# Reordering ScalarE and VectorE work around three places of a decoder trunk: feed of the down projection, Q/K additions, weight sums of the second feed-forward

## The chip, the cores and the metric

The kernel runs on one core of one Trainium2 chip. The metric is the device time of one execution in microseconds (us); the time of a kernel is the median of several runs. TensorE (PE) multiplies matrices and writes into eight banks of PSUM, VectorE (DVE) and ScalarE (ACT) do elementwise work and read those banks, GpSimd (POOL) and SyncE (SP) here mostly issue transfers (DMAs). Each engine runs its own instructions in the order in which the program emitted them and waits on semaphores for the others.

## The reference: what is computed

Two layers on a sequence of 1024 tokens of width 1024, all in float32. Layer 0 mixes tokens with a gated short convolution, layer 1 with a dilated attention of 16 heads (three branches, windows 128, 512 and 2048 with dilation 1, 4 and 16). Each mixer is followed by a SwiGLU feed-forward of inner width 2816, and a norm ends the network:

```python
for i in range(DEPTH):
    h = rms_norm(x, mix_norm[i])
    x = x + (short_conv_mixer if i % 2 == 0 else dilated_attention_mixer)(h, ...)
    h = rms_norm(x, ffn_norm[i])
    x = x + (silu(h @ w_gate[i]) * (h @ w_up[i])) @ w_down[i]
return rms_norm(x, final_norm)
```

## The kernel before

**Precision.** Each float32 operand is split into a high half `hi`, a rounded copy made by ACT, and a low half `lo = t - hi`, a subtraction made by DVE. A product is then three matmuls: hi by hi, hi by lo, lo by hi. Weights are split in `split` (ACT at L147, DVE at L148), activations in `Strassen.hi` (L578, L579) or `operand` (L896, L897). In `Strassen.mm` the matmuls of lines L586, L587 and L588 are the three; L588 is the one that needs the weight's low half.

**Seven products instead of eight.** The large projections use Winograd's form of Strassen's scheme. A unit `u` is a pair of 128-column weight slabs; its products have the numbers m = 1, 2, 6, 5, 7, 3, 4 (`WINOGRAD`). A product (u, m) multiplies a sum of weight blocks (made on DVE by `add_pair`, L208, named `combo`) with operand m, a sum of activation blocks that all units share (tiles `b`). Four pairs of tiles by three make twelve matmuls of 512 columns. The results are collected in banks: ACT saves a bank into a tile `part` (`save`, L592), DVE adds a bank to a tile (`add`, L596). `first(u)` is such an addition; it frees the bank of product (u, 2). Behind the first units of the feed-forward some products go a level deeper (`add_deep`, `deeper`; numbers above `DEEPER`, 256 columns, lines L678 to L681; their sums are L252).

**Order.** The order is written out by hand. `unit_order` lists the products; `products` walks through it. In front of the matmuls of each product `take` emits the splits of the weights of the next two or three products (`ahead`; `ensure` emits up to a given place), and after them come the saves and additions, a hook if there is one, and `filled(n)`, where n is the place in the order. `filled` calls `start(n)` of the stage, which makes the operands and sums at fixed places, then the feed, then `idle`. In the feed-forward the order begins (0,1), (1,1), (0,2), (1,2), (2,1), (2,2), (3,1), (3,2), (0,6), (1,6), (0,7), (1,7), (0,4), (1,4), (0,5), (1,5), (2,6), (0,3), and ends with unit 21: (21,1), (20,3), (21,6), (21,5), (21,7), deep 1, 2, 5, 6, (21,3), deep 7, 3, 4. The last product of a stage is followed by the down projection (`down`).

**Memory.** Large tiles are pages of one pool of 41 (weights, slabs `raw`, operands `b`, loaded tiles `hin`); halves of pages come from a pool of 20. A new tile gets the page that was given back longest ago, and its first writer waits for the last reader of the old tile. Transfers of slabs and `hin` go through SP in order.

**The three places.** (1) `feed(0)` (L774) brings the operands of the first down projection: at each step it allocates and loads three tiles of the next m (L786) and splits the three loaded at the step before (L578 three times, then L579 three times). `run` steps it at four places of the last unit (L864). (2) In `QueryKey.mix` the order begins (0,1), (1,1), (0,2), (1,2), (2,1), (2,2), (3,1), (3,2), (4,1). Behind (1,2) the hook `gather` starts the sums of squares of the norm (ACT L489, DVE L493); behind (3,1) the hook `spread` adds them over the partitions with four matmuls (L501). `first(0)` and `first(1)` are in `start` at n = 3 and 4, each ahead of the weights that `ensure` emits there. (3) `Swiglu.feed_forward` and the output projection before it (`group1` in `into_ffn`). The output projection runs in two halves of columns, j = 0 and 1, each over n = 0 to 7. The sums of weights of unit 0 (`combos[i, 0]`, three DVE instructions for m = 6 and 7) are made in j = 1, those of unit 1 in `start` at n = 0, between the steps of the norm's sums. `second_half` makes the operands of the second half of the sequence in six steps: step 1 multiplies by the norm and makes operands 7 and 6, step 2 subtracts, step 3 makes operand 4, step 4 subtracts, step 5 makes operand 5, step 6 operand 3. After step 1 they are called at n = 5, 7, 8, 10 and 12. The first feed-forward, behind the convolution, has some of these steps at other places, so several numbers depend on `self.key` or `i`, which is 0 for the first feed-forward and 1 for the second.

Of the kernel before, what the change touches and what calls it, by code (L numbers as in the profile page):

```python
# [30 lines left out]
DEEP, DEEPER = (2, 4), 10  # L31
# [72 lines left out]
def trunk(ctx: ExitStack, tc: tile.TileContext, x, gains_in, cwi, ck, cwo, wqkv, wo, relb,  # L104
# [60 lines left out]
    combos, raw_base, sums_of = {}, {}, {}  # L165
# [227 lines left out]
    def run(*gens):  # L393
        for _ in zip(*gens):
            pass
        for g in gens:
            for _ in g:
                pass
# [153 lines left out]
    class Strassen:  # L552
# [292 lines left out]
        def run(self, start, hooks={}):  # L845

            self.base = op_state[1]
            last = self.nu - 1

            def filled(n):  # L850
                start(n)
                if self.key != CONV:
                    self.now = n + 1
                    i = self.order.index((3, 4))
                    if n == i - 10:
                        prep.append(self.deepen(2))
                    if n == i - 1:
                        prep.append(self.deepen(4))
                    for p in prep:
                        next(p, None)  # L860
                if self.key == CONV:
                    self.below(n, last)
                else:
                    if self.order[n] in [(last, m) for m in (1, 6, DEEPER + 1, DEEPER + 4)]:  # L864
                        next(feed, None)
                    if self.order[n] == (last, DEEPER + 7):
                        ensure(self.at(last, DEEPER + 4) + 4)
                self.idle(n)

            prep = []  # L870
            if self.key == CONV:
                self.products(filled, hooks)
                self.first_tiles()
                return
            feed = self.feed(0)
            self.products(filled, hooks)
            for c in range(0, self.pairs, self.chunk):
                self.down(c, 0, feed)
                feed = self.feed(c + self.chunk) if c + self.chunk < self.pairs else self.feed_last()
                self.down(c, 4, feed)  # L880
            run(feed)
# [255 lines left out]
    class QueryKey(Conv):  # L1137
# [43 lines left out]
        def mix(self):  # L1181
            norm = self.norm
            prep = self.differences()
            stats = norm.stats(0, S)
            x12 = []

            def start(n):
                if n == 0:
                    ensure(self.at(2, 2))
                    next(prep)  # L1190
                elif n == 1:
                    ensure(self.at(3, 1))
                    next(prep)
                elif n == 3:
                    self.first(0)
                    ensure(self.at(4, 1))
                elif n == 4:
                    self.first(1)
                    ensure(self.at(4, 2))
                elif n == 5:  # L1200
                    ensure(self.at(0, 6))
                elif n == 6:
                    ensure(self.at(1, 6))
                elif n == 7:
                    next(prep)
                elif n == 8:
                    self.first(2)
                    ensure(self.at(0, 7))
                elif n == 9:
                    next(prep)  # L1210
                    next(prep)
                elif n in (10, 12):
                    next(prep)
                elif n == 11:
                    next(prep)
                    self.first(3)
                elif n == 13:
                    self.first(4)
                elif n == 14:
                    next(prep, None)  # L1220
                elif n == 20:
                    self.ahead = 3

            def gather():
                next(stats)
                next(stats)

            def spread():
                run(stats)
                rms = dram.tile([1, S], F32, name="rms")  # L1230
                norm.r = consts.tile([128, KT], F32, name="scales")
                nc.gpsimd.dma_start(rms, norm.rstd[0:1, :])
                nc.gpsimd.dma_start(norm.r, bass.AP(rms.tensor, rms.offset, [[1, 128], [128, KT]]))
                self.ready = True

            def load():
                for k in range(4):
                    x12.append(half_page("x12"))
                    nc.sync.dma_start(x12[k], spill[k][:, half(1)])

            def last_operand():
                self.b[8] = [None] * 4
                for k in range(4):
                    self.operand(8, k, k, x12[k])

            def filled(n):
                start(n)
                self.idle(n)

            norm.flush()  # L1250
            self.base = op_state[1]
            ensure(self.at(0, 2))
            self.products(filled, {(1, 2): gather, (3, 1): spread, (QK_PAIRS - 1, 1): load, (QK_PAIRS - 1, 7): last_operand})
            self.h = [[self.b[1 + 7 * h * (k < 4) + (1 + h) * (k > 3)][k % 4] for k in range(KT)] for h in range(2)]
            self.step(len(self.waiting) + 1)


    class Swiglu(Strassen):
# [111 lines left out]
        def feed_forward(self, stats, last_step, after, final=None):  # L1370
            prep = []

            def start(n):
                if n == 0:
                    last_step()
                    for m in (6, 7):
                        next(stats)
                        combos[self.key, 1](m)
                    ensure(self.at(3, 1))
                if n == self.key + 1:  # L1380
                    combos[self.key, 2](6)
                    ensure(self.at(0, 6))
                elif n == self.key + 2:
                    run(stats)
                    prep.append(self.second_half())
                    next(prep[0])
                    nc.scalar.activation(scratch, eps, AF.Silu)
                    ensure(self.at(1, 6))
                elif n == 4:
                    ensure(self.at(1, 7))  # L1390
                elif n in (5, 7, 8, 10, 12):
                    next(prep[0], None)
                if n in (8, 24):
                    self.ahead = 3 if n == 8 else 2

            self.run(start)
            key = ("d", self.key)
            if final:
                final(key, self.plain, self.hid)
                return  # L1400
            for n in range(KT):
                add_to_x(n, both(take(key + (n,), 2 if n > 3 else 1), self.plain, self.hid))
                after(n)
# [22 lines left out]
    def into_ffn(i, norm):  # L1426
# [10 lines left out]
        def group1(key, ks, acts):  # L1437
            def added(j, n):

                if j == 0 and n > 2:  # L1440
                    if 3 < n < KT - 2:
                        ensure(op_state[1] + 1)
                    ensure(first_op + n - 2)
                elif j and n in (2, 3):
                    ensure(first_op + n + 4)

            def between(j, n):
                nc.scalar.dma_start(spill[n][:, half(j)], X[n][:, half(j)])
                if j == 0:
                    if n == 2:  # L1450
                        load_raw(raw_base[i] + 3)
                    elif n == 3:
                        if not i:
                            nc.scalar.activation(less, gains, AF.Copy, scale=-1.0)
                    elif n == 4 and last_part:
                        last_part.pop()()
                    elif n == KT - 1:
                        norm.flush()
                    return
                if n == i:  # L1460
                    pre.append(norm.stats(0, HALF))
                    for m in (6, 7):
                        next(pre[0])
                        combos[i, 0](m)
                elif n == i + 1:
                    run(pre.pop())
                    pre.append(sw.first_half())
                for k in (((), (0,), (1,), (2, 3), (4,)), ((), (), (0, 1), (2, 3), (4,)))[i][n] if n < 5 else (n,):
                    step(k)

            by_columns((key, 1), ks, acts, HALVES, lambda n, c: norm.chained(n, *c, i), between,
                       AO_WIDE if key == "ao" else 4, added=added)

# [593 lines left out]
```

## Time and profile before

| what | value |
|---|---|
| median of 3 runs | 2099.22 us (2099.01 to 2099.78) |
| the profiled execution | 2098.44 us |
| its span, first to last instruction | 2096.6 us |
| granted clock of TensorE | 0.999 |
| busy: PE, DVE, ACT, POOL | 99%, 84%, 49%, 12% of the span |
| DMA | 300.72 MB, mean 143 GB/s |

Busy times are shares of the span. In a timeline a row gives the start, the duration from the first to the last instruction merged into it, engine, line, operation, tiles written and read, shape, the count, and in brackets the idle time of the engine before it and what ended it. Instructions of one engine overlap a little, so the count times the pitch, not times the duration of one, gives the time of a row. In the table of waits a row gives who waited for whom, the sum in us, how often, and the longest. A row of the table of stretches gives the stretch, its length, and for each engine the busy time and the number of instructions in it, then clock, share of the DMA engines and GB/s.

### The profile page before, as it was taken

Reading aid. Unit: us, or ns where it says so; the run is one execution under the profiler, and the core shown is the slowest. Engines: PE = TensorE matmul, PEld = TensorE weight load, DVE = VectorE, ACT = ScalarE, POOL = GpSimd, SP = SyncE. Lnnn points to the kernel's source line nnn. Section 1 sums busy time; section 2 is a strip of 40 time slices with the busy share of each in tenths; the row PEclk is TensorE's granted clock in tenths of the full one; section 3 lists DMA queues with packets and bytes.
Section 4 is the critical chain, followed back from the end, with each engine's and each line's share of the span. In section 5 each row is a group of like instructions: output and inputs, shape, how many; then the busy total and the mean of one; then the engine's idle time right before and its main releaser. Section 6 shows DMA issues by size and latency. Waiting matters only on the chain.

```text
span 2096.6 us, 30790 instructions
## 1 busy us (share of the span) xinstructions
PE 2076.3 (99%) x10978; PEld 1788.3 (85%) x10978; DVE 1757.3 (84%) x3308; ACT 1022.6 (49%) x1892; POOL 247.4 (12%) x352
## 2 busy tenths in 40 slices
PE   9999999999999999999999999999999999999998
PEld 7788888888888888888889999998788888888887
DVE  8898769988888788968985888987998888888886
ACT  8333427444444455445544666665544434456433
POOL 1000000110101010010223333211001011001000
PEclk9999999999999999999999999999999999999999
DMA  7232643233333467451656867955222333359432
GB/s 221 96 96 71 231 136 76 105 102 111 103 103 111 143 201 209 135 171 55 227 191 196 218 171 218 244 182 141 76 91 101 106 106 106 116 189 246 159 96 81
DMA packets 124729, 300.72 MB, mean 143 GB/s; under 512 B 15084, under 2 KB 37694, under 8 KB 124576
## 3 DMA queue, kind: packets, MB, share of 16 engines
q1 hardware_dynamic: 90720, 201.94, 31.6%
q0 software_dynamic: 26224, 82.11, 12.6%
q10 hardware_dynamic: 7632, 14.70, 1.9%
q8 instruction: 87, 1.43, 0.3%
q14 instruction: 66, 0.54, 0.1%
HBM read 208.42 MB, written 82.93 MB: 139 GB/s over the span
## 4 chain that ended last, share of the span: by engine, by line
PE 50%; DVE 3%; ACT 1%; issue 0%; DVEq 0%; ACTq 0%
PE bank L588 9%; PE bank L586 9%; PE bank L587 9%; PE bank L1664 5%; PE bank L388 2%; PE bank L390 2%; PE bank L389 2%; PE bank L1533 2%; PE bank L1535 1%; PE bank L1534 1%; PE bank L1590 1%; PE bank L1589 1%; PE bank L678 1%; PE bank L681 1%; PE bank L680 1%; DVE w L148 1%
## 5 line engine op out<-in xcount | busy, mean ns | idle before, releaser
L588 PE MATMUL bank<-b,w 128*128 128x512 f32 x2008 | 782.4, 390 | 4.6 <-DVE w L148 4.4
L586 PE MATMUL bank<-b,w 128*128 128x512 f32 x2008 | 782.5, 390 | 3.9 <-ACT w L147 1.6
L587 PE MATMUL bank<-b,w 128*128 128x512 f32 x2008 | 782.2, 390 | 0.3 <-DVE b L897 0.3
L588 PEld LDWEIGHTS bank<-b,w 128*128 128x128 f32 x2008 | 377.0, 188 | 87.1 <-DVE w L148 8.9
L586 PEld LDWEIGHTS bank<-b,w 128*128 128x128 f32 x2008 | 377.2, 188 | 82.0 <-ACT w L147 3.3
L587 PEld LDWEIGHTS bank<-b,w 128*128 128x128 f32 x2008 | 377.2, 188 | 77.5 <-DVE b L897 1.3
L147 ACT ACTIVATE w<-combo 128x512 fp32r<-128x512 f32 (+2 forms) x496 | 253.9, 542 | 234.5 <-DVE combo L208 217.3
L148 DVE TENSOR_TENSOR w<-combo,w 128x512 fp32r<-128x512 f32 (+2 forms) x496 | 282.3, 582 | 39.3 <-ACT w L147 38.5
L592 ACT ACTIVATE part<-bank 128x512 f32<-128x512 f32 x192 | 114.4, 596 | 395.7 <-PE bank L588 393.2
L148 DVE TENSOR_TENSOR w<-raw,w 128x512 fp32r<-128x512 f32 (+2 forms) x348 | 193.0, 575 | 33.8 <-ACT w L147 33.8
L596 DVE TENSOR_TENSOR part<-part,bank 128x256 f32<-128x256 f32 (+1 forms) x372 | 175.0, 500 | 35.5 <-PE bank L588 18.4
L147 ACT ACTIVATE w<-raw 128x512 fp32r<-128x512 f32 (+2 forms) x348 | 170.6, 532 | 46.0 <-PE bank L588 12.2
L388 PE MATMUL bank<-w_hi,w 128*128 128x512 f32 (+1 forms) x400 | 151.3, 378 | 0.1
L390 PE MATMUL bank<-w_hi,w 128*128 128x512 f32 (+1 forms) x400 | 149.3, 373 | 0.7 <-DVE w L148 0.7
L389 PE MATMUL bank<-w_lo,w 128*128 128x512 f32 (+1 forms) x400 | 149.1, 373 | 0.0
L816 DVE TENSOR_TENSOR x<-x,bank 128x512 f32<-128x512 f32 x136 | 92.7, 682 | 28.4 <-PE bank L588 28.4
L208 DVE TENSOR_TENSOR combo<-raw 128x512 f32<-128x512 f32 (+1 forms) x176 | 113.9, 648 | 0.0
L507 DVE TENSOR_TENSOR x<-x,bank 128x512 f32<-128x512 f32 (+1 forms) x104 | 66.6, 644 | 55.8 <-PE bank L390 54.6
L390 PEld LDWEIGHTS bank<-w_hi,w 128*128 128x128 f32 x400 | 75.4, 188 | 14.8 <-DVE w L148 1.6
L579 DVE TENSOR_TENSOR b<-hin,b 128x512 fp32r<-128x512 f32 x126 | 79.4, 685 | 9.4 <-ACT b L578 9.4
L388 PEld LDWEIGHTS bank<-w_hi,w 128*128 128x128 f32 x400 | 75.5, 189 | 12.0 <-ACT w L147 0.5
L389 PEld LDWEIGHTS bank<-w_lo,w 128*128 128x128 f32 x400 | 75.5, 189 | 11.7
(228 smaller groups left out, 3344.4 us busy)
## 6 DMA issues: line engine op xcount, KB each, us to landing
hin<-part SPq DMA_DIRECT2D x126, 256.0 KB, 5.3
raw<-in_ffn_w_gate SPq DMA_DIRECT2D x44, 512.0 KB
raw<-in_ffn_w_up SPq DMA_DIRECT2D x44, 512.0 KB, 3.8
part<-sum POOLq DMA_DIRECT2D x72, 256.0 KB, 2.3
raw<-in_ffn_w_down SPq DMA_DIRECT2D x48, 384.0 KB, 3.8
raw<-in_attn_w_qkv SPq DMA_DIRECT2D x27, 512.0 KB, 3.8
raw<-in_conv_w_in SPq DMA_DIRECT2D x24, 512.0 KB, 3.6
part<-part POOLq DMA_DIRECT2D x36, 256.0 KB, 2.5
```

The costliest lines, as they stand in the source:

```text
L147: nc.scalar.activation(hi, src, AF.Copy)
L148: low = lambda: eng.tensor_tensor(out=lo, in0=src, in1=hi, op=ALU.subtract)
L208: eng.tensor_tensor(out=c, in0=a, in1=b, op=op)
L388: nc.tensor.matmul(b, whi[:, a], ahi[:, s], start=first, stop=False)
L389: nc.tensor.matmul(b, whi[:, a], alo[:, s], start=False, stop=False)
L390: nc.tensor.matmul(b, wlo[:, a], ahi[:, s], start=False, stop=last)
L586: nc.tensor.matmul(b, hi[:, a], bhi, start=start and k == 0, stop=False, skip_group_check=True)
L587: nc.tensor.matmul(b, hi[:, a], blo, start=False, stop=False, skip_group_check=True)
L588: nc.tensor.matmul(b, lo[:, a], bhi, start=False, stop=k == n - 1, skip_group_check=True)
L592: nc.scalar.activation(t, b, AF.Copy)
L596: nc.vector.tensor_tensor(out=t, in0=t, in1=b, op=ALU.add)
L1664: nc.tensor.matmul(view(acc[ih], off, dims), vx[:, u * 192 + 128 * a:u * 192 + 128 * a + 128], rhs, start=first, stop=last)
```

## The change

Nothing is computed differently; instructions are emitted at other places.

- Down projection, both feed-forwards: the second step of the first feed comes behind (20,3) instead of (21,6), one product sooner; the third behind (21,5) instead of deep product 1, two products sooner. The first and the fourth stay.
- Q/K: `first(0)` goes ahead of the steps of the norm's sums in `gather`, `first(1)` right behind them, so ahead of the weights that `start(3)` and `start(4)` emit.
- Second feed-forward: the sums of unit 0 move from j = 1, n = 1 to j = 0, n = 5 and 6 of the output projection; the sums of unit 1 move from n = 0 of the feed-forward to j = 1, n = 1 of the output projection. The steps 3, 4 and 5 of `second_half` come at n = 8, 10 and 11 instead of 7, 8 and 10.

```diff
@@ in Strassen.run, filled @@
-                    if self.order[n] in [(last, m) for m in (1, 6, DEEPER + 1, DEEPER + 4)]:
+                    if self.order[n] in [(last, 1), (last - 1, 3), (last, 5), (last, DEEPER + 4)]:
                         next(feed, None)
@@ in QueryKey.mix, start and gather @@
                 elif n == 3:
-                    self.first(0)
                     ensure(self.at(4, 1))
                 elif n == 4:
-                    self.first(1)
                     ensure(self.at(4, 2))
...
             def gather():
+                self.first(0)
                 next(stats)
                 next(stats)
+                self.first(1)
@@ in Swiglu.feed_forward, start @@
                     for m in (6, 7):
                         next(stats)
-                        combos[self.key, 1](m)
+                        if not self.key:
+                            combos[0, 1](m)
                     ensure(self.at(3, 1))
...
-                elif n in (5, 7, 8, 10, 12):
+                elif n in ((5, 7, 8, 10, 12), (5, 8, 10, 11, 12))[self.key]:
                     next(prep[0], None)
@@ in into_ffn, between @@
                     elif n == KT - 1:
                         norm.flush()
+                    if i and n in (5, 6):
+                        combos[i, 0](n + 1)
                     return
                 if n == i:
                     pre.append(norm.stats(0, HALF))
                     for m in (6, 7):
                         next(pre[0])
-                        combos[i, 0](m)
+                        combos[i, i](m)
```

## Prediction

> **What bounds the kernel now.** I read the page first, then the waits of TensorE (PE), then around each wait the timelines of PE, VectorE (DVE), ScalarE (ACT) and SP.
>
> ```profile
> span 2096.6 us, 30790 instructions
> PE 2076.3 (99%) x10978; PEld 1788.3 (85%) x10978; DVE 1757.3 (84%) x3308; ACT 1022.6 (49%) x1892; POOL 247.4 (12%) x352
> ```
> ```profile
> PE bank L588 <- DVE w L148: 4.4, 6, 1.4
> ...
> PE bank L678 <- DVE part L596: 1.1, 2, 0.5
> ```
>
> PE is the bound and idles 20 of 2096.6 us, so the change can win a few microseconds at most, wait by wait. The waits name DVE: low halves of weights (L148), which PE needs at the third matmul of a product, and additions that read a bank (L596), before which PE may not write it again.
>
> **Part 1: the feed moved in both feed-forwards.** PE in the last unit of the second one (four rows), and of the first:
>
> ```profile
> 1861.11 0.40 PE L586 MATMUL bank<-b,w 128*128 128x512 f32 x1
> ...
> 1862.17 0.50 PE L588 MATMUL bank<-b,w 128*128 128x512 f32 x1 [0.44 <-DVE w L148]
> 1862.52 0.39 PE L586 MATMUL bank<-b,w 128*128 128x512 f32 x1
> ...
> 1865.27 0.36 PE L678 MATMUL bank<-t,w 128*128 128x256 f32 x1 [0.52 <-DVE part L596]
> ```
> ```profile
> 737.44 0.50 PE L588 MATMUL bank<-b,w 128*128 128x512 f32 x1 [0.43 <-DVE w L148]
> ...
> 740.53 0.36 PE L678 MATMUL bank<-t,w 128*128 128x256 f32 x1 [0.54 <-DVE part L596]
> ```
>
> A free-running matmul of 512 columns follows the last after 0.227 us (three in 0.68, a product of twelve in 2.72; the four L501 rows of part 2 show 0.23 each). Product (21,3) starts at 1861.11, so its third matmul is due at 1861.56 and comes at 1862.17: 0.61 lost. The next comes 0.35 later, 0.12 more for the restart. The deep product behind is due at 1861.11 + 2.72 = 1863.83 and starts at 1865.27: with its own restart (0.06) this tail loses 1.5. From 737.44 to 740.53 the first feed-forward shows the same 3.1 us as 1862.17 to 1865.27, so 1.5 again. Why DVE is late:
>
> ```profile
> 1845.69 1.14 ACT L147 ACTIVATE w<-combo 128x512 fp32r<-128x512 f32 x2
> ...
> 1850.61 1.67 ACT L578 ACTIVATE b<-hin 128x512 fp32r<-128x512 f32 x3
> ```
> ```profile
> 1847.63 0.68 DVE L596 TENSOR_TENSOR part<-part,bank 128x512 f32<-128x512 f32 x1
> ...
> 1851.26 1.90 DVE L579 TENSOR_TENSOR b<-hin,b 128x512 fp32r<-128x512 f32 x3 [1.68 <-ACT b L578]
> ...
> 1861.44 0.68 DVE L148 TENSOR_TENSOR w<-combo,w 128x512 fp32r<-128x512 f32 x1
> ...
> 1864.71 1.34 DVE L596 TENSOR_TENSOR part<-part,bank 128x256 f32<-128x256 f32 x3
> ```
> ```profile
> 1841.95 0.32 SPq L786 DMA_DIRECT2D hin<-part  x1
> ```
> ```profile
> hin<-part SPq DMA_DIRECT2D x126, 256.0 KB, 5.3
> ```
>
> DVE idles 1.68 us before the three subtractions of operand m=1 because ACT's copies for them stand behind the save of (21,6), at 1850.61. After this DVE is late until 1866. The change emits the same three copies, three subtractions and three loads one product sooner, after (20,3), and those of m=2 two sooner. On ACT the copies then follow the first of the two L147 at 1845.69: start 1846.2, and the third by 1847.4, when (20,3) frees its page. On DVE the subtractions follow the addition at 1847.63: 1848.2 to 1850.1, 0.60 each.
>
> What they push back: the weight of (21,7). By the order of allocation in the code all 41 pages are taken once the moved feed has its five (36 held after (20,3)), so that weight gets the page of an m=1 tile just split. Its copy on ACT waits for the second subtraction, 1849.5, and its low half ends at about 1850.9. PE needs it at the third matmul of (21,7); with (21,3) at 1861.11 and four deep products between, each twelve matmuls of 256 columns at 0.12, (21,7) starts at 1861.11 - 5.75 - 2.72 = 1852.64, third matmul 1853.1. Slack 2.2. Queued behind that ACT wait are only the save of (21,6), ready at 1850.1, and what follows it. The m=2 copies come at 1851.7, between the weights of deep products 1 and 2, all in time.
>
> Of DVE's 1.68 us all but 0.1 is filled. The low half of (21,3) ends at 1862.12 - 1.57 = 1860.55, 1.0 before PE wants it. The first addition at 1864.71 ends at 1865.12 and PE starts 0.15 later; moved to 1863.55 + 0.15 = 1863.70 it is 0.13 ahead of 1863.83. Both waits go, with little over. SP's queue: the m=2 loads start about 0.7 sooner, the m=6 loads about 3; the down weights behind them come at most 1.5 later and are split at 1860. Free. The third m=1 load is issued at 1841.95; at the median of 5.3 it lands at 1847.3, when ACT wants it. Bounds: -1.5 (waits gone) to 0 (it lands so late that DVE is where it was) per tail. I take -1.5 twice, since the slacks are counted row by row: **-3.0**.
>
> **Part 2: additions ahead of weights in Q/K.** No instruction is added; first(0) passes two subtractions (L493), first(1) the weights (L148).
>
> ```profile
> 980.27 1.09 PE L501 MATMUL bank<-sum,ones_r 128*128 128x512 f32 x4
> 982.26 0.47 PE L586 MATMUL bank<-b,w 128*128 128x512 f32 x1 [0.90 <-DVE part L596]
> ```
> ```profile
> 1010.58 0.50 PE L588 MATMUL bank<-b,w 128*128 128x512 f32 x1 [0.42 <-DVE w L148]
> ```
> ```profile
> 979.64 0.68 DVE L596 TENSOR_TENSOR part<-part,bank 128x512 f32<-128x512 f32 x1
> 980.24 1.28 DVE L148 TENSOR_TENSOR w<-raw,w 128x512 fp32r<-128x512 f32 x2
> 981.44 0.68 DVE L596 TENSOR_TENSOR part<-part,bank 128x512 f32<-128x512 f32 x1
> ...
> 992.49 1.41 DVE L897 SCALAR_TENSOR_TENSOR b<-x,gains,b 128x512 fp32r<-128x512 f32 x2
> 994.67 1.41 DVE L897 SCALAR_TENSOR_TENSOR b<-x,gains,b 128x512 fp32r<-128x512 f32 x2 [0.77 <-ACT b L896]
> ```
> ```profile
> 993.43 0.60 ACT L592 ACTIVATE part<-bank 128x512 f32<-128x512 f32 x1 [1.29 <-PE bank L588]
> ```
>
> The second addition goes from 981.44 to 980.24, ends at 980.92 and frees the bank. PE then goes on right behind the four L501 matmuls, at 980.27 + 0.91 = 981.18 instead of 982.26: 1.08, and 0.06 for the restart. The pushed work: both sums' low halves end 0.60 later (the second at 980.32, wanted by the fourth L501 at 980.96), the first weight too (981.52, wanted at 981.63). So PE gains 1.14 here, but not for good: at 1010.58 it waits for DVE, whose one gap on the way there is the 0.77 before 994.67, and it hangs on PE: ACT's copy stands behind the save at 993.43. With the save 1.14 sooner DVE starts at 993.83, when the second instruction of the row before, which ends at 993.90, lets it in: 0.84. That is what is left at 1010.58; PE's wait there grows by 0.3. Bounds 0 and -1.14; I take **-0.85**.
>
> **Part 3: second feed-forward, sums sooner and two operands later.** Three sums (L208) of unit 0 go to the end of the first half of the output projection, those of unit 1 to where unit 0's were:
>
> ```profile
> L208 DVE TENSOR_TENSOR combo<-raw 128x512 f32<-128x512 f32 (+1 forms) x176 | 113.9, 648 | 0.0
> ```
> ```profile
> 1428.48 0.69 DVE L507 TENSOR_TENSOR x<-x,bank 128x512 f32<-128x512 f32 x1 [2.03 <-PE bank L390]
> ...
> 1466.19 2.50 DVE L1299 TENSOR_TENSOR x<-x,rstd 128x512 f32<-128x512 f32 x4 [0.95 <-ACT rstd L503]
> ...
> 1501.29 0.68 DVE L596 TENSOR_TENSOR part<-part,bank 128x512 f32<-128x512 f32 x1
> ```
> ```profile
> 1466.19:1502.11 35.92, 34.45 (x150) 27.65 (x149) 35.82 (x60) 23.56 (x42) 1.69 (x3) 1.00 0.16 58
> ```
> ```profile
> 1481.52 0.50 PE L586 MATMUL bank<-b,w 128*128 128x512 f32 x1 [0.40 <-ACT part L592]
> ```
> ```profile
> 1478.54 2.44 ACT L578 ACTIVATE b<-hcol 128x512 fp32r<-128x512 f32 x4 [1.34 <-DVE hcol L1299]
> 1480.89 0.58 ACT L592 ACTIVATE part<-bank 128x512 f32<-128x512 f32 x1
> ```
> ```profile
> 1488.80 0.50 PE L588 MATMUL bank<-b,w 128*128 128x512 f32 x1 [1.07 <-DVE w L148]
> ```
> ```profile
> 1502.11 0.47 PE L586 MATMUL bank<-b,w 128*128 128x512 f32 x1
> ```
>
> Two of the sums (1.3 us) fit into the idle 2.03 before 1428.48, the third follows that addition; the slab load that comes with them is issued sooner, and PE waits for none of it. What leaves the stretch ahead of 1466.19 only lengthens the 0.95 of idle there, because DVE waits for the norm, which PE's order sets. From 1466.19 on DVE has 35.82 of 35.92 us to do, all of it still there. Moving step 3 (operand m=4) behind product (0,6) lets ACT save that bank at 1478.4, when the product ends, instead of behind four copies at 1480.89, so the wait at 1481.52 goes (0.56 + 0.11); the weight wanted at 1488.80 comes before step 4's four subtractions, so this wait goes too (1.23 + 0.11). PE is 2.0 ahead until (2,6). But at 1502.11, product (0,3), PE may not write its bank before the addition at 1501.29 has ended (1501.97 + 0.14). All of DVE's 60 instructions up to there stay before it, only in another order. What is late next: the low half of (2,6), with 0.7 of wait, and then that bank. Sum **0**, from -2.0 (if the bank did not bind) to +0.2 (a restart more).
>
> **The sum.** -1.5 - 1.5 - 0.85 + 0 = -3.85. The profiled execution took 2098.44 (span 2096.6 and 1.84 around it), 0.8 under the median of 2099.22; 2098.44 - 3.85 = 2094.6 for such an execution, 2099.22 - 3.85 = **2095.4** for the median: 0.18% faster.
>
> The Trainium skill has another rule for the restarts ("TensorE: Matmul & The Clock Gate", Part 1): PE's clock falls to half only after an idle window of about 3.4 us. No wait here is that long, so by the rule the restarts cost nothing and the gain would be 3.4; the rows show 0.12 and 0.06 for a restart, and decide.
>
> **Rivals.** (a) Part 3 pays as well: the waits at 1481.52 and 1488.80 go and nothing takes their place: 2095.4 - 2.0 = 2093.4. For it speak the two waits; against it the full DVE. (b) Only the tails pay, or one tail and Q/K: 2096.2 to 2097. For it speak the slacks of 0.11 and 0.13. (c) Waits only change their place in all parts, as in part 3: 2099.2. Against it: DVE has real idle time to fill in parts 1 and 2. (d) Slower: the moved copies of m=1 wait for their load, and ACT cannot pass them: the weight of (21,7), the save of (21,6) and all behind stand still. From 1841.95 a landing up to 7.6 us costs nothing (1847.4 + 2.2); it decides against the change beyond 9.5 (1.9 lost in each of two tails); at twice the median, 10.6, PE loses 3.0 twice and the gain of the tails: 2099.2 + 6.0 - 0.85 = 2104.4. Against it: a median of 5.3.
> The Trainium skill says under "Architectural detail" of the same page that ScalarE and VectorE take their queue strictly in order; ACT's rows around 1850 agree, and (d) hangs on that.
>
> **How the numbers follow.** The forecast has 0.60, (a) 0.12, (b) 0.17, (c) 0.05, (d) 0.06. A measurement tells 0.2%, 4.2 us, from no change: faster means under 2095.0. That is (a) and about 0.2 of the forecast's 0.60, which lies 0.4 from the line: 0.33. Slower, over 2103.4: (d), 0.06. The rest, 0.61, is within. The range 2093.4 to 2097.4 leaves out (c), (d) and a little of the others.
>
> **What would show it.** Tails: no wait of (21,3) on L148 nor of a deep product on L596; the three L579 of m=1 at about 1848 in old time, with no 1.68 before them. Q/K: no wait behind the L501 matmuls, the 0.77 on DVE nearly gone, the later wait on L148 at 0.7 instead of 0.42. Second feed-forward: no wait on L592, one on L148 or a bank at (2,6) or (0,3), DVE as full as before. I am wrong if the moved copies wait for a load or a page, if DVE's order holds other gaps, or if another bank binds first.

## The result, and the profile after

The changed kernel takes 2095.32 us (median of 19 runs, 2094.27 to 2097.78) against 2099.33 for the kernel before (19 runs, 2098.51 to 2100.97): a ratio of 0.9982 with a 95% interval of 0.9974 to 0.9989. That is 4.0 us less where 3.85 was forecast, and a median of 2095.3 where 2095.4 was.

The profiled execution of the changed kernel was one of its longer ones (2097.12). The head of its page:

```profile
span 2095.3 us, 30793 instructions
PE 2077.0 (99%) x10978; PEld 1790.3 (85%) x10978; DVE 1756.8 (84%) x3308; ACT 1023.0 (49%) x1892; POOL 246.7 (12%) x352
```

The span is only 1.3 us under that of before (2096.6). TensorE runs the same 10978 matmuls in the same order in every kernel of this document, so the time between the starts of two given matmuls can be compared trace by trace. The table does that; the columns are named by the times of the matmuls in the profile of before, and each number is the difference to that profile in us. "Median" is the kernel's median less that of the kernel before in the same comparison (2099.33, then 2099.24, 2099.47 and 2099.59).

| kernel | 0 to 339 | to 939 (first feed-forward) | to 990 (Q/K) | to 1025 (Q/K) | to 1160 | to 1510 (second feed-forward begins) | to the end (its tail) | median |
|---|---|---|---|---|---|---|---|---|
| changed | +2.25 | -1.50 | -1.12 | +0.23 | +0.52 | -0.02 | -1.48 | -4.01 |
| e12_again | +0.85 | -1.48 | -1.12 | +0.26 | +0.54 | -0.02 | -1.49 | -3.66 |
| e1_feed | +0.73 | -1.48 | 0.00 | +0.01 | +0.01 | 0.00 | -1.49 | -3.08 |
| e2_qk | +0.36 | -0.05 | -1.10 | +0.21 | +0.25 | +0.01 | -0.02 | -1.24 |
| e3_ffn2 | +1.19 | 0.00 | -0.02 | +0.02 | +0.04 | -0.01 | -0.02 | -0.37 |
| e4_m1_only | +0.84 | -0.30 | 0.00 | +0.01 | +0.16 | +0.01 | -0.32 | -0.43 |
| e11_m2_only | +0.52 | +0.04 | +0.01 | +0.01 | +0.99 | -0.02 | 0.00 | +0.32 |
| e10_late_loads | +0.19 | -1.52 | -1.12 | +0.25 | +0.68 | +0.03 | -1.20 | -3.69 |
| e5_steps | +0.49 | +0.01 | +0.01 | +0.03 | +0.02 | +0.03 | 0.00 | -0.85 |
| e6_dose | -0.04 | -1.48 | -1.07 | +0.21 | 0.00 | +1.23 | -1.48 | -3.20 |
| e7_put_off | +0.66 | -1.48 | -1.07 | +0.19 | +0.23 | -1.15 | -1.48 | -5.34 |
| e8_qk_gap | +0.71 | -1.48 | -1.14 | -0.34 | +0.50 | +0.02 | -1.49 | -4.91 |
| e9_both | -0.16 | -1.48 | -1.12 | -0.36 | +0.08 | -1.22 | -1.44 | -5.90 |

In the five stretches that the change touches, the changed kernel's profile has -1.50 - 1.12 + 0.23 - 0.02 - 1.48 = -3.89, and the second profile (e12_again) -3.85. The +2.25 and +0.52 lie where no code was changed; the second profile of the same kernel has +0.85 and +0.54 there, the other kernels anything from -0.16 to +1.19 and from 0.00 to +0.99, and the last section takes them up. So the table's stretches, and not the two spans, carry the argument; the medians, each over 7 to 33 runs, agree with the sum of the five stretches within 1 us.

The waits of TensorE in the changed kernel (us in total, times, longest):

```profile
PE bank L588 <- DVE w L148: 3.9, 4, 2.0
...
PE bank L586 <- DVE part L596: 1.1, 1, 1.1
```

The line of L678 is gone: no deep product waits for an addition any more. L588 waits 4 times instead of 6, and its 3.9 us hold a wait of 2.0 at the start of the kernel, which was 1.4 before. The L596 wait of 1.1 is another one than the 0.9 of before. The rows of TensorE, in the order of time (Q/K, the start of the second feed-forward, its tail):

```profile
981.01 1.10 PE L501 MATMUL bank<-sum,ones_r 128*128 128x512 f32 x4
981.94 0.40 PE L586 MATMUL bank<-b,w 128*128 128x512 f32 x1
...
1010.46 0.50 PE L588 MATMUL bank<-b,w 128*128 128x512 f32 x1 [0.65 <-DVE w L148]
...
1498.84 0.50 PE L588 MATMUL bank<-b,w 128*128 128x512 f32 x1 [0.53 <-DVE w L148]
...
1502.53 0.47 PE L586 MATMUL bank<-b,w 128*128 128x512 f32 x1 [1.14 <-DVE part L596]
...
1861.48 0.40 PE L586 MATMUL bank<-b,w 128*128 128x512 f32 x1
...
1861.95 0.39 PE L588 MATMUL bank<-b,w 128*128 128x512 f32 x1
...
1864.01 0.39 PE L588 MATMUL bank<-b,w 128*128 128x512 f32 x1
1864.23 0.28 PE L678 MATMUL bank<-t,w 128*128 128x256 f32 x1
```

Product (21,3) starts at 1861.48, its third matmul follows 0.47 later, and the deep product 0.22 after the last matmul: no wait is left. In Q/K the product goes on 0.93 after the first L501, with no wait, and the later wait has grown from 0.42 to 0.65. In the second feed-forward two waits stand at new places. VectorE and ScalarE beside them:

```profile
991.42 1.89 DVE L947 TENSOR_TENSOR x<-x 128x512 f32<-128x512 f32 x3
993.23 2.73 DVE L897 SCALAR_TENSOR_TENSOR b<-x,gains,b 128x512 fp32r<-128x512 f32 x4
...
1498.10 0.68 DVE L148 TENSOR_TENSOR w<-combo,w 128x512 fp32r<-128x512 f32 x1
...
1499.30 1.28 DVE L1358 TENSOR_TENSOR part<-part 128x512 f32<-128x512 f32 x2
...
1501.71 0.68 DVE L596 TENSOR_TENSOR part<-part,bank 128x512 f32<-128x512 f32 x1
...
1848.01 0.68 DVE L596 TENSOR_TENSOR part<-part,bank 128x512 f32<-128x512 f32 x1
1848.60 1.89 DVE L579 TENSOR_TENSOR b<-hin,b 128x512 fp32r<-128x512 f32 x3
1850.41 0.68 DVE L148 TENSOR_TENSOR w<-combo,w 128x512 fp32r<-128x512 f32 x1
...
1853.30 1.89 DVE L579 TENSOR_TENSOR b<-hin,b 128x512 fp32r<-128x512 f32 x3
...
1857.12 0.68 DVE L664 TENSOR_TENSOR c<-part,bank 128x512 f32<-128x512 f32 x1
...
1860.25 0.68 DVE L148 TENSOR_TENSOR w<-combo,w 128x512 fp32r<-128x512 f32 x1
...
1863.52 0.74 DVE L596 TENSOR_TENSOR part<-part,bank 128x256 f32<-128x256 f32 x2
```
```profile
1846.07 0.62 ACT L147 ACTIVATE w<-combo 128x512 fp32r<-128x512 f32 x1
1846.59 1.87 ACT L578 ACTIVATE b<-hin 128x512 fp32r<-128x512 f32 x3
1848.45 0.63 ACT L147 ACTIVATE w<-combo 128x512 fp32r<-128x512 f32 x1
1850.49 0.60 ACT L592 ACTIVATE part<-bank 128x512 f32<-128x512 f32 x1 [1.41 <-PE bank L588]
```

The three subtractions of m=1 follow the addition at 1848.01 with no idle time before them, and those of m=2 come at 1853.30, ahead of L664 instead of behind it. In the kernel before they stood there:

```profile
1856.50 0.68 DVE L664 TENSOR_TENSOR c<-part,bank 128x512 f32<-128x512 f32 x1
...
1859.03 1.88 DVE L579 TENSOR_TENSOR b<-hin,b 128x512 fp32r<-128x512 f32 x3
```

The busy time of each engine over the start of the second feed-forward (stretch, its length, then PE, PEld, DVE, ACT and POOL busy, with the number of instructions):

```profile
1466.60:1502.50 35.90, 34.27 (x150) 27.71 (x150) 35.79 (x60) 23.39 (x42) 1.68 (x3) 1.00 0.17 55
```

VectorE has 35.79 of 35.90 us to do, in 60 instructions, as before.

### The profile page after: what moved, and what is told of

Read it like the earlier page. It is cut to its first block, busy times and chain, and to the rows that moved or that the text cites. A ratio compares the mean times of both kernels' runs of the same rounds, so it can differ in the third digit from the quotient of the medians.

```text
span 2095.3 us, 30793 instructions
## 1 busy us (share of the span) xinstructions
PE 2077.0 (99%) x10978; PEld 1790.3 (85%) x10978; DVE 1756.8 (84%) x3308; ACT 1023.0 (49%) x1892; POOL 246.7 (12%) x352
## 4 chain that ended last, share of the span: by engine, by line
PE 91%; DVE 4%; ACT 1%; issue 1%; DMA 0%; DVEq 0%; SPq 0%; ACTq 0%
PE bank L588 20%; PE bank L586 20%; PE bank L587 20%; PE bank L1667 5%; PE bank L390 4%; PE bank L388 4%; PE bank L389 4%; PE bank L681 3%; PE bank L680 3%; PE bank L678 3%; PE bank L1536 2%; PE bank L1538 1%; PE bank L1537 1%; PE bank L1593 1%; PE bank L1592 1%; DVE b L579 1%
## 5 line engine op out<-in xcount | busy, mean ns | idle before, releaser
L588 PE MATMUL bank<-b,w 128*128 128x512 f32 x2008 | 782.9, 390 | 4.1 <-DVE w L148 3.9
L588 PEld LDWEIGHTS bank<-b,w 128*128 128x128 f32 x2008 | 377.4, 188 | 85.9 <-DVE w L148 7.6
L596 DVE TENSOR_TENSOR part<-part,bank 128x256 f32<-128x256 f32 (+1 forms) x372 | 174.8, 498 | 35.8 <-PE bank L588 18.8
```

Of the source, the lines that this page charges most:

```text
L588: nc.tensor.matmul(b, lo[:, a], bhi, start=False, stop=k == n - 1, skip_group_check=True)
L596: nc.vector.tensor_tensor(out=t, in0=t, in1=b, op=ALU.add)
```

## The experiments

All kernels but one issue the same instructions in another order; e6_dose has two more, whose results nobody uses.

**The change in three.** Each part of the diff alone, on the kernel before. The feed:

```diff
-                    if self.order[n] in [(last, m) for m in (1, 6, DEEPER + 1, DEEPER + 4)]:
+                    if self.order[n] in [(last, 1), (last - 1, 3), (last, 5), (last, DEEPER + 4)]:
```

> Only the feed of the down projection is moved, in both feed-forwards; Q/K and the start of the second feed-forward stay as before. My theory: both tails lose their two waits and nothing else moves, 1.5 us each, so 3.0 us less than before (2096.3 for a median of 2099.3); from the last matmul before 339.04 us (the sums' matmul in the first feed-forward's norm) to 939.05 us TensorE needs 598.5 instead of 600.0. Rival: the parts depend on each other and the gain of the whole change comes mostly from the other two parts: then this kernel gains under 2 us.

Measured 2096.16 against 2099.24, ratio 0.9986 (0.9978 to 0.9995); 1.48 and 1.49 less in the two tails, nothing elsewhere behind 339. Q/K alone:

```diff
             def gather():
+                self.first(0)
                 next(stats)
                 next(stats)
+                self.first(1)
```

> Only the two additions of Q/K pass the weights; all else as before. My theory: the wait of 0.90 at 982.26 goes, 1.14 us, but VectorE sets the later wait at 1010.58, so only 0.85 stays: 2098.5 for a median of 2099.3, and the wait at 1010.58 grows from 0.42 to 0.65 or 0.7. Rival one: the wait gone is a full gain, 1.14, and the later wait stays at 0.42. Rival two: all is given back at 1010.58, 0, with a later wait of about 1.5.

Measured 2098.00 against 2099.24, ratio 0.9994 (0.9986 to 1.0003), which by itself can't tell 0.85 from 1.14. The trace can: 1.10 less up to 990, 0.21 given back up to 1025, 0.89 in all, and the wait at 1010 is 0.64. The start of the second feed-forward alone:

```diff
-                elif n in (5, 7, 8, 10, 12):
+                elif n in ((5, 7, 8, 10, 12), (5, 8, 10, 11, 12))[self.key]:
...
-                        combos[i, 0](m)
+                        combos[i, i](m)
...
+                    if i and n in (5, 6):
+                        combos[i, 0](n + 1)
```

> Only the start of the second feed-forward is changed: three sums earlier and two operands later. My theory: 0 (-0.2 to +0.3): the two old waits (0.40 and 1.07 us, with restarts 1.9 us) go, and two new ones of the same sum stand at the third matmul of (2,6) and at the first of (0,3), because VectorE does the same work without a pause up to the addition that frees that bank. Rival: the waits go for good and the kernel is 1.9 us faster.

Measured 2098.87 against 2099.24, ratio 0.9997 (0.9988 to 1.0006), and -0.01 from 1160 to 1510. The three parts add up: -2.97, -0.89 and -0.01 make -3.87, and the whole change has -3.89.

**Which step of the feed pays.** Only the second step (m=1) moved, and then only the third (m=2):

```diff
-                    if self.order[n] in [(last, m) for m in (1, 6, DEEPER + 1, DEEPER + 4)]:
+                    if self.order[n] in [(last, 1), (last - 1, 3), (last, DEEPER + 1), (last, DEEPER + 4)]:
```

> Of the feed, only the second step is moved (copies and subtractions of operand m=1, and the loads of m=2, to behind (20,3)); the third step (copies and subtractions of m=2) stays where it was, behind the first deep product. All else as before. My theory: the place of the m=1 copies on ScalarE is what made VectorE late, so this alone gives the whole 3.0 us (1.5 in each tail), the third step's move is worth nothing (within 0.3). Rival: the two steps share the gain, and this kernel still waits at the deep product behind (21,3): 1 to 2 us of gain.

Measured 2098.81 against 2099.24, ratio 0.9997 (0.9989 to 1.0006): 0.30 and 0.32 less in the tails, a fifth of the 1.5 expected. My theory fell. VectorE in that kernel:

```profile
1854.99 0.76 DVE L148 TENSOR_TENSOR w<-combo,w 128x256 fp32r<-128x256 f32 x2
1856.91 0.69 DVE L664 TENSOR_TENSOR c<-part,bank 128x512 f32<-128x512 f32 x1 [1.17 <-ACT part L592]
...
1859.45 1.89 DVE L579 TENSOR_TENSOR b<-hin,b 128x512 fp32r<-128x512 f32 x3
...
1861.86 0.68 DVE L148 TENSOR_TENSOR w<-combo,w 128x512 fp32r<-128x512 f32 x1
```

The idle time of 1.68 before m=1 is gone, but VectorE, early now, runs into L664, which needs the save of (21,7), and that comes when TensorE has done that product. It idles 1.17 there (and 0.19 at an earlier row), and the subtractions of m=2 stand behind L664 as they did. Of 1.68 us, 0.3 is left. The rest needs work that may be done before the save of (21,7), and that is m=2, moved by the third step.

```diff
-                    if self.order[n] in [(last, m) for m in (1, 6, DEEPER + 1, DEEPER + 4)]:
+                    if self.order[n] in [(last, 1), (last, 6), (last, 5), (last, DEEPER + 4)]:
```

> The kernel before with only the third step of the feed moved (copies and subtractions of m=2, to behind (21,5)); those of m=1 stay behind (21,6). After the run with only the second step moved, which gained 0.3 per tail and showed a new idle time of 1.17 on VectorE before L664 (it waits for the save of (21,7)), my theory is that VectorE has two places to idle, one behind the other, and the third step fills the second one: alone it does nothing, since the first idle time of 1.68 stays: 2099.3, waits of 0.43 and 0.53 in each tail as before. Rival: the third step is the part that pays: 1.2 us per tail, 2096.9.

Measured 2099.91 against 2099.59, ratio 1.0002 (0.9992 to 1.0011), and +0.04 and 0.00 in the tails: alone the third step is worth nothing, as the new theory says. I was wrong about the places. VectorE, TensorE and ScalarE there:

```profile
1852.82 1.90 DVE L579 TENSOR_TENSOR b<-hin,b 128x512 fp32r<-128x512 f32 x3 [1.69 <-ACT b L578]
```
```profile
1862.28 0.35 PE L678 MATMUL bank<-t,w 128*128 128x256 f32 x1 [0.90 <-ACT w L147]
```
```profile
1861.23 1.86 ACT L147 ACTIVATE w<-combo 128x512 fp32r<-128x512 f32 x5 [2.38 <-DVE combo L208]
```

The 1.69 is still there, and TensorE waits for a high half: ScalarE stands 2.38 at a weight whose sum comes from the late VectorE, and the weights of the deep products are queued behind it. The same lateness shows at another place.

**The price of a late load.** The loads of m=1 behind those of m=2 in SP's queue:

```diff
-                    for k in range(self.chunk):
+                    for k in range(self.chunk if c or m != 1 else 0):
                         nc.sync.dma_start(new[k], self.parts[c + k, m])
+                    for k in range(0 if c or m != 2 else self.chunk):
+                        nc.sync.dma_start(tiles[k], self.parts[c + k, 1])
```

> The changed kernel with the three loads of operand m=1 behind those of m=2 in SP's queue, so that the third is issued at about 1846 instead of 1842.3 and lands some 3.4 us later, at about 1851. This measures the price of the rival that the moved copies wait for their load. By the prediction's rule (free up to 7.6 us after 1941.95's like, 1841.95, the rest lost in each tail) a landing at 8.9 loses 1.3 in each tail: 2.6 slower than the changed kernel, 2097.9. Rival one: ScalarE's wait costs nothing because VectorE has other work meanwhile: 2095.3. Rival two: ScalarE holds up all the weights behind it and the tails lose the full 3.4 each: 2102.

Measured 2095.90, and 2095.93 for the changed kernel beside it: no slower by the medians. The dose was smaller than I had meant. Rows of ScalarE and TensorE:

```profile
1843.20 0.60 ACT L592 ACTIVATE part<-bank 128x512 f32<-128x512 f32 x1 [1.60 <-PE bank L588]
...
1846.51 2.03 ACT L578 ACTIVATE b<-hin 128x512 fp32r<-128x512 f32 x3 [1.68 <-DMA hin<-part]
```
```profile
1862.15 0.39 PE L588 MATMUL bank<-b,w 128*128 128x512 f32 x1
1862.58 0.36 PE L678 MATMUL bank<-t,w 128*128 128x256 f32 x1
```

The copies now do wait for their loads, 1.68 us. Counted from the save before them (1843.20 here, 1845.05 in the changed kernel), the last of the three ends at 5.34 instead of 3.41, so 1.9 later and not 3.4. The prediction allowed 2.2 without loss (1847.4 + 2.2, its landing at 7.6), so this dose lies below its turning point. The first tail lost nothing; the second lost 0.28, since its deep product, whose slack was the smallest, starts 0.43 behind the matmul before it instead of 0.22. So the price below the turning point is 0 to 0.3 in a tail, not quite the nothing that was forecast; what lies beyond it, and with it the price of a slower kernel in rival (d), was not tried.

**Whether VectorE is the bound at the start of the second feed-forward.** First the steps without the sums, on the kernel before:

```diff
-                elif n in (5, 7, 8, 10, 12):
+                elif n in ((5, 7, 8, 10, 12), (5, 8, 10, 11, 12))[self.key]:
```

> The kernel before, with only the two operand steps of the second feed-forward one product later (5, 8, 10, 11, 12); its sums stay where they were. My theory: the sums are worth nothing, so this does what both together did: no wait at 1481.5 and 1488.8, waits of 0.53 at the third matmul of (2,6) and 1.13 at the first of (0,3), sum 0 (within 0.3). Rival: the earlier sums are what kept VectorE from being later still, and without them the two new waits are longer by up to 1.8 us (three sums of 0.60).

Measured 2098.62 against 2099.47, ratio 0.9995 (0.9986 to 1.0004), and +0.03 in the stretch, with waits of 0.54 and 1.09 at the two new places. The earlier sums are worth nothing. Then a dose, on the changed kernel:

```diff
+                elif n == 9 and self.key:
+                    for _ in range(2):
+                        t = half_page("part")
+                        nc.vector.tensor_tensor(out=t, in0=X[0][:, half(0)], in1=X[0][:, half(1)], op=ALU.add)
```

> The changed kernel with two additions more on VectorE (half rows of x, results used by nobody), placed behind the ninth product of the second feed-forward, at about 1487 us. My theory: VectorE has no slack from the norm up to the addition that frees the bank of (0,3), so both show in full: 2 x 0.60 = 1.2 us slower than the changed kernel, with 1.2 us more of waiting between 1486 and 1503. Rival: the bank wait at (0,3) is not set by how much VectorE has to do (a late release, another engine), and the two additions cost less than 0.4.

Two more instructions cost 1.23 - (-0.02) = 1.25 in the stretch, 0.62 each (median 2096.27). The wait at (2,6) took all of it, 1.74 for 0.53, and that at (0,3) stayed:

```profile
1497.29 0.50 PE L588 MATMUL bank<-b,w 128*128 128x512 f32 x1 [1.74 <-DVE w L148]
...
1500.98 0.47 PE L586 MATMUL bank<-b,w 128*128 128x512 f32 x1 [1.09 <-DVE part L596]
```

Then the order, with no instruction more or less:

```diff
         def idle(self, n):
...
                 self.silus.pop(key)[1]()
+            if self.key and n == 13:
+                return
```

> The changed kernel with the same work in another order: in the second feed-forward the two multiplications of L1358 that come in front of the addition which frees the bank of (0,3) (at 1499.30 and 1499.90) are put behind it. My theory: that addition ends 1.2 us sooner, the wait of 1.13 at (0,3) goes with its restart, so 1.1 to 1.3 us less than the changed kernel; the wait of 0.53 at (2,6) stays. Rival: as before, the wait moves on to the next product (the bank of (1,3), or a weight), and nothing is gained.

Measured 2094.13 against 2099.47, ratio 0.9973 (0.9963 to 0.9984). VectorE and TensorE:

```profile
1498.68 0.68 DVE L596 TENSOR_TENSOR part<-part,bank 128x512 f32<-128x512 f32 x1
1499.27 1.29 DVE L1358 TENSOR_TENSOR part<-part 128x512 f32<-128x512 f32 x2
```
```profile
1497.01 0.50 PE L588 MATMUL bank<-b,w 128*128 128x512 f32 x1 [0.53 <-DVE w L148]
...
1499.51 0.47 PE L586 MATMUL bank<-b,w 128*128 128x512 f32 x1
```

The addition stands before the multiplications, the wait at (0,3) is gone and comes back nowhere: -1.15 in the stretch where the changed kernel has -0.02. So the waits of part 3 were not a fixed sum; it was the order in front of one bank that kept them.

**The later wait in Q/K.** VectorE's other idle time, 2.56 us before 986.60, filled with subtractions that stood behind it. It stands in the kernel before as well:

```profile
985.87 0.69 DVE L148 TENSOR_TENSOR w<-combo,w 128x512 fp32r<-128x512 f32 x1 [2.55 <-ACT w L147]
```

The edit, on the changed kernel:

```diff
-            los = [self.hi(7, k, t3[k]) for k in range(4)]
-            for lo in los:
-                lo()
-            yield
+            def seven():
+                for lo in [self.hi(7, k, t3[k]) for k in range(4)]:
+                    lo()
...
+            if self.key != CONV:
+                seven()
+                yield
...
                 elif n == 5:
+                    next(prep)
                     ensure(self.at(0, 6))
...
-                elif n in (10, 12):
+                elif n == 12:
```

> The changed kernel with, in Q/K, the four subtractions of L947 moved from 990.8 into VectorE's idle time of 2.56 us before 986.60, and the last two copies and subtractions of operand m=5 (L896, L897) one product sooner. My theory: the wait at 1010.46 (0.65) hangs on VectorE's order alone and goes when that idle time is filled: 0.7 us less than the changed kernel, no more than 1.2 (with the two short waits at 1013.59 and 1024.80). Rival: between 990 and 1005 VectorE waits for ScalarE and TensorE again, the time is given back, and the wait at 1010 stays: within 0.2 of the changed kernel.

Measured 2094.56 against 2099.47, ratio 0.9975 (0.9965 to 0.9985); Q/K has -1.48 in place of -0.89. VectorE (of the four moved subtractions, L950, the first is not in this view) and TensorE:

```profile
982.45 1.89 DVE L950 TENSOR_TENSOR x<-x 128x512 f32<-128x512 f32 x3
...
989.31 2.74 DVE L897 SCALAR_TENSOR_TENSOR b<-x,gains,b 128x512 fp32r<-128x512 f32 x4
992.68 0.69 DVE L148 TENSOR_TENSOR w<-combo,w 128x512 fp32r<-128x512 f32 x1 [0.63 <-ACT w L147]
```
```profile
1008.33 0.50 PE L588 MATMUL bank<-b,w 128*128 128x512 f32 x1
```

Part of the time goes into new idle times of VectorE, 0.63 in the last row and 0.90 before 998.12, and 0.59 reaches TensorE: its wait fell from 0.65 to 0.07, the two short ones behind it stayed.

**A version that beats both.** The last two together:

> The changed kernel with both reorderings: the two multiplications put off in the second feed-forward (1.25 us less in its own run's profile: the wait at (0,3) went) and the four subtractions of Q/K in VectorE's idle time (0.55 less: the wait at 1010 went from 0.65 to 0.07). My theory: the two lie 480 us apart and add up: 1.8 us less than the changed kernel, 2093.5 for 2095.3. Rival: what one gains the other loses again at a common later wait: 2094.1 as with the first alone.

Measured 2093.69 us (8 runs) against 2099.59 for the kernel before, ratio 0.9972 (0.9962 to 0.9983), and 2095.93 for the changed kernel beside it. The two gains stand next to each other in the table (-0.36 and -1.22): 1.2 + 0.6 = 1.8 us under the changed kernel by the traces, 2.2 by the medians.

**The changed kernel once more.**

> The changed kernel once more, on the same chip as the three others, for a second profile: 2095.3. In the stretch from 25 to 65 us, where neither the code nor any theory here differs between the kernels, I expect waits of 1.5 to 2 us at about 25 and 59 and, behind one of them, matmuls at about half pace for some 3 us, as in the other profiles but the first one of the kernel before.

Measured 2095.93 against 2099.59, ratio 0.9982 (0.9973 to 0.9990). The stretches of the change came out as in the first profile, within 0.03. The last sentence was a miss: the waits are there (1.57 and 2.02), the slow matmuls are not.

## Why the prediction was right, step by step

- **Part 1, the tails** (-3.0): -1.50 and -1.48. The rows lie where they were forecast. In the second tail the changed kernel's profile is 0.38 later than that of before (the save of (21,1) at 1845.05 instead of 1844.67). The subtractions begin at 1848.60 - 0.38 = 1848.22 (1848.2 forecast). The low half of (21,3) ends at 1860.93, 1.0 before TensorE uses it. The first addition of the pair at 1863.52 ends 0.41 later (the x2 row less the 0.33 between two) and with 0.15 to the release leaves 0.15 up to 1864.23, where 0.13 was forecast.
- **A step that failed in its reason:** "Why DVE is late" named one idle time, the 1.68 before m=1, and the move of m=2 was listed as merely "all in time". e4_m1_only and e11_m2_only show that one move gives 0.3 and the other nothing. A second idle time of 1.17 stands behind the first, hidden as long as VectorE is late. The sum came out because the change has both moves; that the second one fills this idle time is nowhere in the prediction, and e4_m1_only was expected to give the whole 3.0, so in this respect the -3.0 was luck. The question "what is late next" was put for the first idle time to TensorE's needs only, and not to VectorE's own next wait.
- **A detail that failed without cost:** the weight of (21,7) did not wait for the page of an m=1 tile. Its copy starts at 1848.45, right behind the third L578, 1.0 sooner than forecast even before the 0.38 is taken off.
- **Part 2, Q/K** (-0.85): -1.12 + 0.23 = -0.89, and -0.89 alone. The 0.77 before the second pair of L897 has closed (one row of four at 993.23), and the later wait is 0.65 where "0.7 instead of 0.42" was said. One reading was incomplete: the 0.77 is not VectorE's "one gap on the way there". The 2.55 before 985.87 lies on it too. It ends with a weight on ScalarE that stands behind the steps of the norm (L502, L503) and so behind the L501 matmuls, which did not move; the gap stayed (2.56), and the sum with it. That it could be filled, for 0.59, only e8_qk_gap shows.
- **Part 3** (0): -0.02. "The low half of (2,6), with 0.7 of wait, and then that bank": 0.53 and 1.14. The sums are worth nothing (e5_steps), the count of VectorE's work decides (e6_dose). Rival (a) is out for this order of instructions. But the zero hung on the order in front of that bank: e7_put_off has 1.15 of rival (a)'s 2.0 by taking two instructions out from in front of the bank's addition. "All of DVE's 60 instructions up to there stay before it" was the step that carried the zero, and it is the one to attack.
- **The restarts:** with 0.12 and 0.06 for each the forecast was 3.85, without them 3.4. The five stretches of the two profiles, 3.89 and 3.85, stand with the rows. The medians give 4.0 and, in the second comparison, 3.7, so it is partly chance that the first lies within 0.2 of the forecast. The Trainium skill's rule ("TensorE: Matmul & The Clock Gate", Part 1) is one on the clock, which is to fall to half after an idle window; the prediction read from it that restarts cost nothing, but it does not speak of them. Here the granted clock was 1.00 from 1861.5 to 1863 in the kernel before, and the matmul after the wait at 1862.17 still came 0.35 later instead of 0.227.
- **The rivals.** (b) and (c) are excluded by the stretches: both tails and Q/K paid what was forecast. (d) did not happen: the third copy had ended at 1848.46 and ScalarE idled 1.41 before the save of (21,6). e10_late_loads shows the mechanism at work (ScalarE 1.68 at the copies) and its price at that dose. The Trainium skill's statement that ScalarE takes its queue strictly in order (same page, "Architectural detail") agrees with that run and with the 2.38 of e11_m2_only, where weights stood behind one that waited.

## What to carry to other kernels

When an idle time of a busy engine is to be filled, follow that engine's own queue to its next wait: moved work only pays if what now comes sooner does not stand at the next release, and a second idle time can be hidden behind the first. Where an engine is full up to an instruction that frees a buffer, count the instructions in front of that one; an instruction that nobody needs so soon, put behind it, was worth 0.6 us each here, while moving waits about in front of it was worth nothing. And where a change is worth less than the run to run difference of an untouched stretch, compare the same matmuls' times in both traces, not the spans.

## What the runs showed of the hardware

The stretch from 0 to 339 us, the same code everywhere, differed by 2.4 us between the profiles (-0.16 to +2.25). One part of it is TensorE's clock. The traces first record it in full 4.0 to 10.7 us after the start, and it can fall again later. The wait at 59 us in the changed kernel's first profile and in its second (e12_again):

```profile
59.43 0.80 PE L588 MATMUL bank<-b,w 128*128 128x512 f32 x1 [2.03 <-DVE w L148]
60.02 0.63 PE L586 MATMUL bank<-b,w 128*128 128x512 f32 x1
```
```profile
59.60 0.50 PE L588 MATMUL bank<-b,w 128*128 128x512 f32 x1 [2.02 <-DVE w L148]
59.94 0.40 PE L586 MATMUL bank<-b,w 128*128 128x512 f32 x1
```

And the busy times of 3.4 us from there on, in the same two (the granted clock is the third number from the right):

```profile
59.40:62.80 3.40, 3.37 (x8) 2.69 (x9) 3.40 (x6) 1.36 (x3) 0.00 (x0) 0.50 0.54 154
```
```profile
59.55:62.95 3.40, 3.35 (x15) 2.74 (x15) 3.40 (x6) 1.39 (x3) 0.00 (x0) 1.00 0.51 154
```

The same wait to 0.01 us, and once the clock fell to a half for about 3.4 us (8 matmuls where there are 15), once it did not. In 8 of the 14 profiles there is one such stretch, seven times from about 27 us, behind waits of 1.6 to 2.0 at 25 and 0.67 at 26.5. A matmul of 512 columns then starts every 0.43 us instead of 0.227, and a stretch costs up to some 1.6 us (8 x 0.20 in e2_qk). The Trainium skill speaks of a free-running window of about 3.4 us (same page, Part 1): the length agrees, and a window whose phase is not the kernel's would explain why equal waits end differently. That an idle window is needed for it does not agree: 2.0 us of waiting were enough here.

The clock records of the traces say more. In all 8 the fall comes a whole number of steps of 3.413 us after the first record of full clock (6 steps, 20.48 us, seven times; 16 steps, 54.61 us, in the changed kernel's first profile) and lasts one step. Counted in these steps, the one before each fall holds 1.65 to 2.23 us of idle time of TensorE. Up to the last matmul no step with less than 1.65 was followed by a fall, and of those with more three were not: 1.74 (e6_dose), 1.75 (e7_put_off) and 1.86 (e12_again, where the end of the step cuts the wait of 2.02). So about half a step of idle time decided, not sharply by this count, and where the wait lay in the steps is what parted the two profiles above. Behind the waits that this change touches or makes (up to 1.14), and behind the 1.74 of e6_dose, no profile shows one.

The +0.52 between 1025 and 1160 differs from profile to profile as well, but not by the clock: a matmul at about 1139 waits between 0 and 0.70 us from profile to profile; in the four where the trace names a cause (e8_qk_gap, e10_late_loads, e11_m2_only, e12_again) it is a load of the attention's weights. Counted from the matmul at 1025, that load is issued at the same time in all 14 (1132.1 to 1132.6 in the times of before), whether or not the kernel is ahead there; so the load moves with TensorE, and nothing shows that the wait takes back a part of the gain.
